# Expert weights read in runs of 8192 bytes, and eight instead of four weight pieces loaded ahead of the routing, in other memory

## The chip, the core and the metric

One Trainium2 chip, one of its cores. The metric is the device time of one execution in microseconds (us). One core has a matrix engine (TensorE: PE in the rows, PEld its weight loads), a vector engine (DVE), a scalar engine (ACT), GpSimd (POOL), and a sync engine (SP), whose queue here only issues DMAs. DMAs of SP and ACT, and those of POOL, run on 16 DMA engines; the rows call SP's queue q1, ACT's q10 and POOL's q0.

## What is computed

A decoder block for 512 tokens of width 1024 in float32: a mixer (a state-space branch and a block-sparse attention branch, merged by gates), then a layer of 32 experts of which each token uses four. Only the second half and its beginning matter here:

```python
h2 = (rms_norm(x, ffn_pre_g[l]) * (1.0 + sc_f) + sh_f).astype(dtype)
logits = hf @ router_w + router_b
top_val, top_idx = lax.top_k(logits, TOP_K)          # 4 of 32 experts
top_w = jax.nn.softmax(top_val, axis=-1)
g = xb @ w_gate[e] + b_gate[e]                       # xb: an expert's tokens
u = xb @ w_up[e] + b_up[e]
g = jnp.minimum(g, SWIGLU_LIMIT)
u = jnp.clip(u, -SWIGLU_LIMIT, SWIGLU_LIMIT)
act = g * jax.nn.sigmoid(SWIGLU_ALPHA * g) * (u + 1.0)
y = act @ w_down[e] + b_down[e]                      # summed per token, times top_w
```

Each of the three matrices of an expert is 1024 x 1024 in float32, 4 MB; the 32 experts together have 403 MB, and every one of them is read once.

## The kernel before

**Stages.** The mixer runs first, up to the output projection with `w_out`. That projection reads the merged branches from `hTh` and `hTl` (two tiles of 16 KB in each of the 128 partitions, in which the modulated input had lain; the pool `front`) and `w_out` itself, split into high and low parts in the tiles `hi` and `lo` (pool `split`, four buffers of each, 4 KB in a partition). Then come the residual (written to `x1d` in HBM by POOL), the modulated input of the experts (`hs`, written to `h2d` by POOL), the router, the top four, and the lists of tokens per expert. Then the expert stage.

**Expert stage.** Each expert is a *slot*. The order of slots is written out in `ORDER`; letters stand for the number of token places that a slot has room for: q is 32, h 64, m 64 + 32, w 128, b 128 + 32 or 128 + 64 (three b, two w, nine each of m, h and q). The first two slots are q slots of experts 0 and 1, whatever the routing says; all others take the expert with a given rank by number of tokens, whose number the SP queue reads from the tile `eid` (`Slot.weight`) once the routing is known.

**Pieces.** A 4 MB matrix is read in four *pieces* of 1 MB, each 256 rows: partition p gets row 256q + p and row 256q + 128 + p, that is two runs of 4096 bytes. `Stream` hands the pieces out in the order in which TensorE wants them (`jobs`): gate and up of slot 0, gate of slot 1, down of slot 0, up of slot 1, gate of slot 2 and so on, 384 pieces in all. Pieces 0 to 19 belong to experts 0 and 1. A piece goes to one of 11 ring buffers in turn (`big_chunk`): buffers 0 to 2 are pairs of tiles of 4 KB from the pool `ring` and take two DMAs of 512 KB each; buffers 3 to 6 (`ring2`), 7 and 8 (`ring3`) and 9 and 10 (`ring4`) are one tile `[128, 2, 1024]` and take one DMA of 1 MB. Line 1134 issues the former, line 1138 the latter. `Stream.get` refills a buffer when its piece has been used.

**Ahead of the routing.** Four pieces, at the places in `PLACES`, are loaded by `early_chunk` (line 1145) into tiles that the wide slots use only later (`EARLY` names them; they come from the pool `slot`, which reuses the memory of the stages before). Nine more go to ring buffers 0 to 8; the two in `ring3` are issued by POOL. The two buffers of `ring4` lie where tiles of the routing lay, so their loads wait for those.

**Use of a piece.** For a slot with at most 64 places the piece is TensorE's moving operand at full precision (line 1287), 32 places working in four column groups side by side, 64 in two. For 128 places it is split into high and low parts by ACT and DVE (lines 110, 111) and multiplied in three passes (lines 115 to 117). The other operand holds the slot's tokens, gathered from `h2d` by an indirect DMA of POOL (`xg`, line 1225) and transposed by TensorE, 128 columns at a time (`Slot.transposed`, lines 1245 and 1255); the activations before `w_down` are transposed in the same way. Results are added to `yd` in HBM by an indirect DMA of POOL (line 1331).

**The end.** `yd` and `x1d` are read back, normed, and written out.

Of the kernel before, what the change touches and what calls it, by code (L numbers as in the profile page):

```python
# [8 lines left out]
F32 = mybir.dt.float32  # L9
F32R = mybir.dt.float32r  # L10
# [7 lines left out]
P = 128  # L18
D = 1024
SEQ = 512  # L20
NT = SEQ // P
DC = D // P
# [12 lines left out]
HALF = P // 2  # L35
# [12 lines left out]
RINGS = 11  # L48
FIRST = 9
MIX = "aagaasstt"  # L50
PLACES = (0, 1, 3, 4)
LOADS = 1
PRIO = 300
EARLY = (("s128", "u128"), ("xh", "xl"), ("ah", "al"), ("xg128", "yo128"))
ALPHA = 1.702
LIMIT = 7.0
SILU_MAX = ALPHA * LIMIT / (1.0 + math.exp(-ALPHA * LIMIT))
# [13 lines left out]
def tile_hybrid_block(ctx: ExitStack, tc: tile.TileContext, A, out):  # L71
    nc = tc.nc
    vec, act, pool, pe = nc.vector, nc.scalar, nc.gpsimd, nc.tensor
# [3 lines left out]
    split = ctx.enter_context(tc.tile_pool(name="split", bufs=4))  # L77
# [9 lines left out]
    def mm_tile():  # L87
        return psum.tile([P, 512], F32, name="mm", tag="mm", bufs=4)

    def ax_tile():  # L90
        return psum.tile([P, 512], F32, name="ax", tag="ax", bufs=3)
# [72 lines left out]
    ident = cst.tile([P, P], F32, name="ident")  # L164
# [354 lines left out]
    for a in range(8):  # L519
        pt = ax_tile()[:64]  # L520
# [3 lines left out]
        for b in range(2):  # L524
            o = U[64 * b:64 * b + 64, 4 * a:4 * a + 4]
# [367 lines left out]
    pos_fix = keep.tile([P, NT, NFIX], F32, name="pos_fix")  # L893
# [130 lines left out]
    for m in (32, HALF):  # L1024
        c = part_col[m] = mo.tile([P, 1], F32, name=f"part{m}")
# [22 lines left out]
    for kh in range(2):  # L1048
        ws = w_chunk(wov, 0, kh)
        for k in range(4):  # L1050
            kk = 4 * kh + k
            for i in range(NT):
                c = slice(i * P, (i + 1) * P)
# [34 lines left out]
    for i in range(NT):  # L1088
        p = mm_tile()
        c = slice(i * P, (i + 1) * P)  # L1090
# [3 lines left out]
    with tc.manual_schedule(engines={vec.engine}):  # L1094
        for c in STEPS.split():
            i = int(c[1])
# [7 lines left out]
    fr.close()  # L1104
    fps.close()

    slp = ctx.enter_context(tc.tile_pool(name="slot", bufs=1, side="right", reuse_waits="tile"))
    ring3 = ctx.enter_context(tc.tile_pool(name="ring3", bufs=FIRST - 7, side="right", reuse_waits="tile"))

# [8 lines left out]
    def tr_tile():  # L1118
        return mps.tile([P, 512], F32, name="tr", tag="tr", bufs=2)
# [20 lines left out]

    def early_chunk(src, tags, eng):

        w = [slp.tile([P, D], F32, name="early", tag=t) for t in tags]
        for k in range(2):
            eng.dma_start(w[k], src[:, k])
        return w
# [4 lines left out]
    def parts_of(m):  # L1151
        return P // m if m <= HALF else 1

    def sized(name, m):

        w = D // parts_of(m)
        return slp.tile([P, w], F32, name=f"{name}{m}", bufs=2 if m <= HALF and name != "u" else 1)

    class Slot:

        def __init__(self, rank, blocks, expert=None):
            self.rank, self.blocks, self.e, self.pick = rank, blocks, expert, None
            if isinstance(expert, int):
                self.pick = own[:, expert:expert + 1].to_broadcast([3 * E + 1, P])
            self.whole = any(m > HALF for m in blocks)
            self.small = any(m <= HALF for m in blocks)
            self.x, self.xg, self.idx, self.w, self.oh = [], [], [], [], []

        def weight(self, name, q):
            if self.e is None:
                self.e = nc.sync.value_load(eid[0:1, self.rank:self.rank + 1], min_val=0, max_val=E - 1)
            w = A[name][0]
            w = w[self.e:self.e + 1] if isinstance(self.e, int) else w[bass.ds(self.e, 1)]
            return w.rearrange("o (k p) n -> p (o k) n", p=P)[:, 2 * q:2 * q + 2]

        def places(self):
            at_ = 0
            place = pos[:, :, self.rank:self.rank + 1] if self.e is None else pos_fix[:, :, self.e:self.e + 1]  # L1180
            for m in self.blocks:
                oh = slp.tile([P, NT, P], BF16, name="oh", bufs=2)
                n = parts_of(m)
                shp = [P, NT, n, m]
                vec.tensor_tensor(oh[:, :, :n * m].rearrange("p i (n m) -> p i n m", n=n),
                                  iota_s[:, None, None, at_:at_ + m].to_broadcast(shp),
                                  place[:, :, None, :].to_broadcast(shp), op=ALU.is_equal)
                self.oh.append(oh[:, :, :n * m])
                at_ += m
# [48 lines left out]
        def transposed(self, t, name, m):  # L1238
            if m <= HALF:
                n = P // m  # L1240
                c = DC // n
                h = slp.tile([P, DC, m], F32, name=f"{name}t{m}", bufs=2)
                pt = tr_tile()[:, :c * P]
                for j in range(c):
                    pe.transpose(pt[:, j * P:(j + 1) * P], t[:, j * P:(j + 1) * P], ident)  # L1245
                act.activation(h.rearrange("p (n j) t -> p j n t", n=n),  # L1246
                               pt.rearrange("p (j n t) -> p j n t", j=c, n=n), AF.Copy)
                return h, None
            h = slp.tile([P, DC, P], F32R, name=name + "h")[:, :, :m]
            l = slp.tile([P, DC, P], F32R, name=name + "l")[:, :, :m]  # L1250
            for q in range(2):
                pt = tr_tile()[:, :4 * m]
                for k in range(4):
                    c = 4 * q + k
                    pe.transpose(pt[:, k * m:(k + 1) * m], t[:m, c * P:(c + 1) * P], ident[:m, :m])
                pv = pt.rearrange("p (k t) -> p k t", t=m)
                act.activation(h[:, 4 * q:4 * q + 4], pv, AF.Copy)
                vec.tensor_sub(l[:, 4 * q:4 * q + 4], pv, h[:, 4 * q:4 * q + 4])
            return h, l
# [48 lines left out]
        def gate(self, ps):  # L1308
            self.s = []
            for p, m in zip(ps, self.blocks):  # L1310
                s = sized("s", m)
                pv, _, sv = self.shaped(p, s, m)
                act.activation(sv, pv, AF.Silu, scale=ALPHA)
                self.s.append(s)
# [20 lines left out]
    class Stream:  # L1335
# [7 lines left out]
        def load(self, tags=None, at_=0, eng=None):  # L1343
            slot, name, q = self.todo.pop(at_)
            w = slot.weight(name, q)
            if tags:
                return slot, 0, early_chunk(w, tags, eng or nc.sync)
            self.live += 1
            return slot, 1, big_chunk(w, eng or nc.sync)
# [45 lines left out]
    with tc.high_priority(PRIO):  # L1395
        parts = {n: stream.load(t, n - i) for i, (n, t) in enumerate(zip(PLACES, EARLY))}

# [13 lines left out]
    rank = rtp.tile([E, 1], F32, name="rank")  # L1411
# [16 lines left out]
    pos = mo.tile([P, NT, E], F32, name="pos")  # L1428
# [17 lines left out]
    pt = tr_tile()  # L1446
# [74 lines left out]
    with tc.For_i(0, n_more, 1):  # L1521
        hit = slp.tile([P, E], F32, name="hit")
        j = slp.tile([P, E], F32, name="hit_j")
# [43 lines left out]
        nc.sync.dma_start(y[:, 0], yd[i * P:(i + 1) * P])  # L1567
    sums, r = [], []
    for i, y in enumerate(ys):
        j = slp.tile([P, D], F32, name="yj", tag=("s128", "yo128")[i % 2])  # L1570
        if i % 2 == 0:
            sums.append(slp.tile([P, 2], F32, name="fs", bufs=2))
        act.activation(j, y[:, 0], AF.Square, accum_out=sums[-1][:, i % 2:i % 2 + 1])
# [30 lines left out]
```

## Time and profile before

| | us |
|---|---|
| median of 3 runs (1586.89 to 1588.97) | 1587.94 |
| the profiled execution | 1585.03 |
| its span, first to last instruction | 1583.2 |
| PE busy in the span | 1400.6 |
| DVE, ACT, POOL busy | 666.3, 441.1, 232.9 |
| DMA queue of SP (q1), share of 16 engines' span | 75.5% |

Busy times are sums over the whole span; the stages have different limits, and a busy PE is not a PE at its peak, since its matmuls are pipelined and a record may last while the next is already running. The DMA share of a stretch can go over 1.00, because an engine's next packet starts a little before the last one ends. HBM was read at 319 GB/s on average over the span; from about 520 us on, where the experts run, it is about 400.

### The profile page before, as it was taken

The page shows a single profiled execution, that of the slowest core. Times are in us where ns is not written, and L with a number is a line of the kernel's source. Part 1 is how long each engine was busy: PE and PEld are TensorE (multiplying, and loading weights), DVE is VectorE, ACT ScalarE, POOL GpSimd, SP SyncE. Part 2 cuts the span into 40 slices and gives each one's busy share as a digit, 9 for nine tenths or more (in the row PEclk, how much of TensorE's full clock was granted, in tenths as well). Part 3 has the DMA queues.
Part 4 walks back from the last instruction along what each step waited for, and adds up shares of the span by engine and source line. Part 5 has one row for each costly group of instructions (what it writes and reads, how often), then busy time and mean ns, then how long its engine had stood idle before and what let it go on. Part 6 is the DMA issues. An engine that isn't in the chain of part 4 may idle for free. (4 is left out here: it accounts for less than half of the span.)

```text
span 1583.2 us, 25206 instructions
## 1 busy us (share of the span) xinstructions
PE 1400.6 (88%) x9746; PEld 748.1 (47%) x9746; DVE 666.3 (42%) x1435; ACT 441.1 (28%) x715; POOL 232.9 (15%) x241
## 2 busy tenths in 40 slices
PE   6999898899895899799999979997998999999871
PEld 3877676556673433233543336435533556333220
DVE  4697898586746210113431025304512556111003
ACT  4444343455432101003230123304302344010001
POOL 1000334000335101011011111101110111010101
PEclk9999999899996999999999999998998999899985
DMA  9524554542647999999999999999999999999995
GB/s 317 164 67 158 175 184 137 172 157 90 222 176 263 377 405 399 397 404 400 403 343 399 394 401 406 397 400 400 395 402 400 406 394 402 395 397 403 401 404 202
DMA packets 160458, 506.96 MB, mean 320 GB/s; under 512 B 18789, under 2 KB 21481, under 8 KB 160079
## 3 DMA queue, kind: packets, MB, share of 16 engines
q1 hardware_dynamic: 140208, 461.04, 75.5%
q0 software_dynamic: 11456, 26.81, 6.4%
q10 hardware_dynamic: 8670, 17.46, 3.2%
q8 instruction: 78, 1.28, 0.3%
q14 instruction: 46, 0.37, 0.1%
HBM read 481.93 MB, written 23.33 MB: 319 GB/s over the span
## 5 line engine op out<-in xcount | busy, mean ns | idle before, releaser
L1287 PE MATMUL acc<-raw,xt 128*32 128x256 f32 (+1 forms) x3712 | 467.7, 463 | 43.7 <-DMA raw<-in_w_up 22.2
L1287 PEld LDWEIGHTS acc<-raw,xt 128*32 128x32 f32 (+1 forms) x3712 | 145.4, 119 | 295.4 <-issue 200.7
L1287 PE MATMUL acc<-raw,at 128*32 128x256 f32 (+1 forms) x1888 | 233.6, 465 | 19.5 <-DMA raw<-in_w_down 19.3
L111 DVE TENSOR_TENSOR lo<-raw,hi 128x1024 fp32r<-128x1024 f32 x170 | 208.3, 1251 | 79.2 <-ACT hi L110 77.6
L110 ACT ACTIVATE hi<-raw 128x1024 fp32r<-128x1024 f32 x170 | 175.7, 1057 | 120.7 <-PE acc L117 36.3
L1321 DVE TENSOR_SCALAR u<-acc 128x256 f32<-128x256 f32 (+2 forms) x44 | 27.6, 628 | 394.8 <-PE acc L1287 373.6
L1331 POOL DMA_INDIRECT yd<-yo,dst x44 | 74.0, 1682 | 562.6 <-ACT yo L1330 458.7
L1287 PEld LDWEIGHTS acc<-raw,at 128*32 128x32 f32 (+1 forms) x1888 | 74.6, 120 | 149.0 <-issue 93.7
L1225 POOL DMA_INDIRECT xg<-h2d,src x44 | 48.8, 1109 | 371.9 <-DVE tb_t L1229 163.0
L1330 ACT ACTIVATE yo<-acc,w 128x256 f32<-128x256 f32 (+2 forms) x44 | 26.9, 636 | 230.6 <-PE acc L1287 197.2
L1246 ACT ACTIVATE at<-tr 128x256 f32<-128x256 f32 (+1 forms) x39 | 18.1, 487 | 251.9 <-PE tr L1245 251.9
L115 PE MATMUL mm<-hTh,hi 128*128 128x512 f32 x192 | 79.1, 416 | 9.5 <-ACT stage L741 7.0
L115 PE MATMUL acc<-hi,xh 128*128 128x512 f32 x160 | 74.5, 465 | 12.6 <-ACT hi L110 12.6
L117 PE MATMUL mm<-hTh,lo 128*128 128x512 f32 x192 | 77.6, 409 | 5.7 <-DVE lo L111 5.7
L116 PE MATMUL mm<-hTl,hi 128*128 128x512 f32 x192 | 78.0, 406 | 0.0
L116 PE MATMUL acc<-lo,xh 128*128 128x512 f32 x160 | 67.1, 419 | 3.8 <-DVE lo L111 3.8
L1246 ACT ACTIVATE xt<-tr 128x256 f32<-128x256 f32 (+1 forms) x39 | 18.0, 487 | 175.3 <-PE tr L1245 175.3
L117 PE MATMUL acc<-hi,xl 128*128 128x512 f32 x160 | 65.7, 410 | 0.0
L255 DVE SCALAR_TENSOR_TENSOR acc<-raw,cond,acc 128x512 f32<-128x512 f32 x56 | 57.1, 1020 | 0.5
L115 PE MATMUL mm<-hi,hTh 128*128 128x512 f32 x128 | 52.6, 415 | 2.2 <-DVE ga L863 1.3
L117 PE MATMUL mm<-hi,hTl 128*128 128x512 f32 x128 | 51.9, 405 | 1.1 <-DVE hTl L308 1.1
L116 PE MATMUL mm<-lo,hTh 128*128 128x512 f32 x128 | 51.6, 403 | 0.0
(577 smaller groups left out, 1815.7 us busy)
## 6 DMA issues: line engine op xcount, KB each, us to landing
raw<-in_w_up SPq DMA_DIRECT2D x97, 1024.0 KB, 16.4
raw<-in_w_gate SPq DMA_DIRECT2D x88, 1024.0 KB, 16.7
raw<-in_w_down SPq DMA_DIRECT2D x88, 1024.0 KB, 16.1
raw<-in_w_down SPq DMA_DIRECT2D x78, 512.0 KB, 15.8
raw<-in_w_gate SPq DMA_DIRECT2D x72, 512.0 KB, 16.4
raw<-in_w_up SPq DMA_DIRECT2D x60, 512.0 KB, 15.8
raw<-in_ada_w SPq DMA_DIRECT2D x48, 512.0 KB, 4.6
raw<-in_w_in SPq DMA_DIRECT2D x32, 512.0 KB, 4.7
```

The costliest lines, as they stand in the source:

```text
L110: act.activation(hv, src, AF.Copy)
L111: eng.tensor_sub(lv, src, hv)
L115: pe.matmul(o, sh, mh, start=start, stop=False)
L116: pe.matmul(o, sh, ml, start=False, stop=False)
L117: pe.matmul(o, sl, mh, start=False, stop=stop)
L255: vec.scalar_tensor_tensor(acc, w[:, k % 2], cond[:, k:k + 1], acc, op0=ALU.mult, op1=ALU.add)
L1225: pool.indirect_dma_start(out=xg[:r], out_offset=None, in_=h2d.rearrange("t (n c) -> (t n) c", n=n), in_offset=bass.IndirectOffsetOnAxis(a ...
L1246: act.activation(h.rearrange("p (n j) t -> p j n t", n=n), pt.rearrange("p (j n t) -> p j n t", j=c, n=n), AF.Copy)
L1287: pe.matmul(o, xh[:, kk], raw[:, c], start=(kk == 0), stop=last)
L1321: vec.tensor_scalar(uv, pv, LIMIT + 1.0, 1.0 - LIMIT, op0=ALU.min, op1=ALU.max)
L1330: act.activation(yv, pv, AF.Copy, scale=w)
L1331: pool.indirect_dma_start(out=yd.rearrange("t (n c) -> (t n) c", n=parts_of(m)), out_offset=bass.IndirectOffsetOnAxis(ap=idx[:, :1], axis= ...
```

## The change

Two parts. First, the rows of a piece are dealt out differently: partition p now gets rows 256q + 2p and 256q + 2p + 1, which are neighbours in HBM, so that a tile of `ring2` to `ring4` is filled by runs of 8192 bytes. Buffers 0 to 2 and the early tiles, which take a row per DMA, keep runs of 4096 bytes. The tokens and the activations are transposed to match: each transpose takes every second column (`rows_of_k`). Second, eight pieces, 3 to 10, are loaded early in place of pieces 0, 1, 3 and 4: four into the `hi` and `lo` tiles, and four into the tiles of the wide slots, which now have a pool of their own, `block`, opened first on the side of the memory where `hTh` and `hTl` lay. The new attribute `fixed` tells the two fixed slots from the others in `places`.

```diff
-PLACES = (0, 1, 3, 4)
+PLACES = (3, 4, 5, 6, 7, 8, 9, 10)
-EARLY = (("s128", "u128"), ("xh", "xl"), ("ah", "al"), ("xg128", "yo128"))
+EARLY = (("hi", "lo"),) * 4 + (("s128", "u128"), ("xh", "xl"), ("ah", "al"), ("xg128", "yo128"))
...
+    blp = ctx.enter_context(tc.tile_pool(name="block", bufs=1, side="right", reuse_waits="tile"))
     slp = ctx.enter_context(tc.tile_pool(name="slot", bufs=1, side="right", reuse_waits="tile"))
...
-        w = [slp.tile([P, D], F32, name="early", tag=t) for t in tags]
+        w = [(split if t in ("hi", "lo") else blp).tile([P, D], F32, name="early", tag=t) for t in tags]
...
+    def rows_of_k(t, m, k):
+        c = 2 * P * (k // 2) + k % 2
+        return t[:m, c:c + 2 * P - 1:2]
...
-            return w.rearrange("o (k p) n -> p (o k) n", p=P)[:, 2 * q:2 * q + 2]
+            return w.rearrange("o (q p c) n -> q p (o c) n", q=4, c=2)[q]
...
-                    pe.transpose(pt[:, j * P:(j + 1) * P], t[:, j * P:(j + 1) * P], ident)
+                    pe.transpose(pt[:, j * P:(j + 1) * P], rows_of_k(t, P, j), ident)
...
-                    pe.transpose(pt[:, k * m:(k + 1) * m], t[:m, c * P:(c + 1) * P], ident[:m, :m])
+                    pe.transpose(pt[:, k * m:(k + 1) * m], rows_of_k(t, m, c), ident[:m, :m])
```

The tiles of 128 places (`s128`, `u128`, `xh`, `xl`, `ah`, `al`, `xg128`, `yo128`) move from `slot` to `block` everywhere else too.

**On SP, where the early pieces are issued.** The first row of each listing is the last ring piece ahead of them. Names after "waits" are what the queue waits for: DMAHW an earlier DMA of SP or ACT, DMASW one of POOL, the others an engine. Before:

```order
123 L1134 DMA raw<-in_w_up 128x1024 [waits DMAHW6_49,DVE_49,Activation_49]
124 L1145 DMA early<-in_w_gate 128x1024 [waits DMASW1_49,DMAHW1_49,DVE_49,DMAHW7_49,PE_49,Activation_49]
125 L1145 DMA early<-in_w_gate 128x1024 [waits DMAHW0_49,DVE_49]
126 L1145 DMA early<-in_w_gate 128x1024 [waits DMASW0_49]
127 L1145 DMA early<-in_w_gate 128x1024 [waits DMAHW2_49,DMASW7_49]
128 L1145 DMA early<-in_w_gate 128x1024 [waits DMAHW3_49]
129 L1145 DMA early<-in_w_gate 128x1024 [waits DMAHW4_49,DVE_49,PE_49]
130 L1145 DMA early<-in_w_up 128x1024 [waits DMAHW5_49,Pool_49]
```

And now:

```order
123 L1136 DMA raw<-in_w_gate 128x1024 [waits DMAHW6_49,DVE_49,Activation_49]
124 L1147 DMA early<-in_w_gate 128x1024 [waits DMAHW7_49,PE_49]
125 L1147 DMA early<-in_w_gate 128x1024 [waits DMAHW0_49,PE_49]
126 L1147 DMA early<-in_w_up 128x1024 [waits DMAHW1_49,PE_49]
127 L1147 DMA early<-in_w_up 128x1024 [waits DMAHW2_49]
128 L1147 DMA early<-in_w_up 128x1024 [waits DMAHW3_49,PE_49]
129 L1147 DMA early<-in_w_up 128x1024 [waits DMAHW4_49]
130 L1147 DMA early<-in_w_up 128x1024 [waits DMAHW5_49,PE_49]
```

DMAs of POOL and the engines DVE, ACT and POOL are gone from the waits; PE is left, beside an earlier DMA of the queue. The early DMAs go on to row 139, sixteen in all.

**On SP, right behind them.** Before, the two pieces for `ring4` (rows 132 and 133) come next, then refills of the ring:

```order
131 L1145 DMA early<-in_w_up 128x1024 [waits DMAHW6_49]
132 L1138 DMA raw_4582<-in_w_down 128x2x1024 [waits DMAHW7_49,DVE_49,PE_49]
133 L1138 DMA raw_4584<-in_w_down 128x2x1024 [waits DMASW4_49,DMASW3_49,DMASW5_49,DMASW2_49,DMASW6_49,DVE_49,DMAHW0_49,PE_49,Activation_49]
134 L1134 DMA raw<-in_w_down 128x1024 [waits DMAHW1_49,PE_49]
135 L1134 DMA raw<-in_w_down 128x1024 [waits DMAHW2_49,PE_49]
136 L1134 DMA raw<-in_w_up 128x1024 [waits DMAHW3_49,PE_49]
```

Now five reads of expert numbers stand ahead (rows 140 to 149), then a refill of ring buffer 0, and only then the two for `ring4`:

```order
148 L1181 TENSOR_LOAD eid
149 L1181 ISA x2
150 L1136 DMA raw<-in_w_up 128x1024 [waits DMAHW7_49,PE_49]
151 L1136 DMA raw<-in_w_up 128x1024 [waits DMAHW0_49,PE_49]
152 L1140 DMA raw_4601<-in_w_up 128x2048 [waits DVE_49,DMAHW1_49,Activation_49,Pool_49]
153 L1140 DMA raw_4603<-in_w_up 128x2048 [waits DMASW3_49,DMASW4_49,DMASW2_49,DMASW5_49,DMASW1_49,DMASW6_49,DMASW0_49,DMAHW2_49,DVE_49,Activation_49]
154 L1136 ISA
```

The first piece for `ring4` has moved behind a DMA that waits for PE. The shape of a 1 MB load, 128x2x1024 before, is 128x2048.

## Rows read from the trace of the kernel before

**Rows 1.** The page, part 2: the span in 40 slices.
```profile
GB/s 317 164 67 158 175 184 137 172 157 90 222 176 263 377 405 399 397 404 400 403 343 399 394 401 406 397 400 400 395 402 400 406 394 402 395 397 403 401 404 202
```
**Rows 2.** DMA queues, 540 to 790 us: packets, MB, share of 16 engines.
```profile
q1 hardware_dynamic: 25260, 95.90, 95.8%
q0 software_dynamic: 2179, 4.33, 6.9%
```
**Rows 3.** SP's waits, 560 to 1550 us: total us, times, longest.
```profile
SPq L1138 <- PE acc L1287: 102.8, 63, 5.6
SPq L1138 <- DMA raw<-in_w_gate: 91.3, 71, 3.8
```
**Rows 4.** PE's groups, 540 to 1550 us: busy us, mean ns, idle before.
```profile
L1287 PE MATMUL acc<-raw,xt 128*64 128x512 f32 x1216 | 302.2, 612 | 19.7 <-DMA raw<-in_w_gate 10.4 <-DMA raw<-in_w_up 9.0
L1287 PE MATMUL acc<-raw,xt 128*32 128x256 f32 x2304 | 159.8, 391 | 21.9 <-DMA raw<-in_w_up 11.1 <-DMA raw<-in_w_gate 10.6
L1287 PE MATMUL acc<-raw,at 128*64 128x512 f32 x608 | 150.2, 615 | 10.4 <-DMA raw<-in_w_down 10.1
L1287 PE MATMUL acc<-raw,at 128*32 128x256 f32 x1200 | 81.9, 392 | 7.9 <-DMA raw<-in_w_down 7.9
```
**Rows 5.** Stretches: busy us of PE, PEld, DVE, ACT, POOL (count), PEclk, DMA share, GB/s.
```profile
805.00:810.00 5.00, 5.00 (x23) 2.78 (x22) 3.06 (x3) 2.01 (x2) 0.00 (x0) 1.00 0.93 355
810.00:815.00 5.00, 5.00 (x22) 2.82 (x21) 0.00 (x0) 0.00 (x0) 0.00 (x0) 1.00 0.76 266
815.00:820.00 5.00, 5.00 (x58) 2.30 (x60) 0.00 (x0) 1.80 (x2) 1.62 (x1) 1.00 0.69 218
```
**Rows 6.** The same view, before and at the start of the expert stage.
```profile
455.00:475.00 20.00, 18.73 (x93) 15.19 (x91) 9.82 (x25) 4.90 (x12) 12.71 (x29) 1.00 0.08 33
...
500.00:515.00 15.00, 8.09 (x52) 4.99 (x52) 6.59 (x34) 1.87 (x6) 3.60 (x4) 0.54 0.71 275
515.00:520.00 5.00, 4.46 (x72) 2.46 (x75) 3.18 (x12) 1.37 (x2) 0.00 (x0) 1.00 0.63 207
```
**Rows 7.** SP's timeline: start us, us, merged issues.
```profile
482.29 11.91 SPq L1145 DMA_DIRECT2D early<-in_w_gate  x6
...
506.83 10.90 SPq L1138 DMA_DIRECT2D raw<-in_w_down  x2
```
**Rows 8.** SP's waits, the whole run.
```profile
SPq L1145 <- DMA x1d<-X: 29.5, 1, 29.5
```
**Rows 9.** PE's timeline: last reading of `hTl`, and the first pieces.
```profile
470.64 0.40 PE L117 MATMUL mm<-hi,hTl 128*128 128x512 f32 x1
...
514.24 1.07 PE L1453 MATMUL tr<-perm,wdT 32*128 32x32 f32 x8
515.24 1.07 PE L1287 MATMUL acc<-early,xt 128*32 128x256 f32 x16
```
**Rows 10.** DMA queues, 16 to 20 us (runs of 2048 bytes).
```profile
DMA packets 810, 1.56 MB, mean 391 GB/s; under 512 B 47, under 2 KB 47, under 8 KB 810
q1 hardware_dynamic: 810, 1.56, 105.4%
```
**Rows 11.** DMA queues, 541 to 551 us (4096 bytes, nearly alone).
```profile
DMA packets 1074, 4.15 MB, mean 415 GB/s; under 512 B 64, under 2 KB 64, under 8 KB 1073
q1 hardware_dynamic: 1073, 4.13, 102.3%
```
**Rows 12.** DMA queues in two loads `sg<-gd`, 299.5 to 301.5, 305 to 307 us.
```profile
q10 hardware_dynamic: 100, 0.82, 100.5%
...
q10 hardware_dynamic: 102, 0.84, 101.3%
```
**Rows 13.** DMA queues, 304.5 to 308 us.
```profile
q10 hardware_dynamic: 132, 0.95, 68.3%
```
**Rows 14.** Transposes of narrow slots (line 1245): ns min/median/max, times.
```profile
L1245 PEld LDWEIGHTS tr<-ident,xg x116: 137/140/224, 509.5 to 1507.9; 128*128 128x128 f32 x116
L1245 PE MATMUL tr<-ident,s x116: 272/273/476, 526.6 to 1540.9; 128*128 128x128 f32 x116
```

More of the change, by code (lines that the diff above doesn't have):

```diff
@@ L1156, in sized @@
         w = D // parts_of(m)
-        return slp.tile([P, w], F32, name=f"{name}{m}", bufs=2 if m <= HALF and name != "u" else 1)
+        return (slp if m <= HALF else blp).tile([P, w], F32, name=f"{name}{m}", bufs=2 if m <= HALF and name != "u" else 1)
+    def rows_of_k(t, m, k):
+        c = 2 * P * (k // 2) + k % 2
+        return t[:m, c:c + 2 * P - 1:2]
     class Slot:
         def __init__(self, rank, blocks, expert=None):
-            self.rank, self.blocks, self.e, self.pick = rank, blocks, expert, None
+            self.rank, self.blocks, self.e, self.fixed, self.pick = rank, blocks, expert, expert, None
             if isinstance(expert, int):
@@ L1175, in weight @@
             w = w[self.e:self.e + 1] if isinstance(self.e, int) else w[bass.ds(self.e, 1)]
-            return w.rearrange("o (k p) n -> p (o k) n", p=P)[:, 2 * q:2 * q + 2]
+            return w.rearrange("o (q p c) n -> q p (o c) n", q=4, c=2)[q]
         def places(self):
             at_ = 0
-            place = pos[:, :, self.rank:self.rank + 1] if self.e is None else pos_fix[:, :, self.e:self.e + 1]
+            place = pos[:, :, self.rank:self.rank + 1] if self.fixed is None else pos_fix[:, :, self.fixed:self.fixed + 1]
             for m in self.blocks:
@@ L1248, in transposed @@
                 return h, None
-            h = slp.tile([P, DC, P], F32R, name=name + "h")[:, :, :m]
-            l = slp.tile([P, DC, P], F32R, name=name + "l")[:, :, :m]
+            h = blp.tile([P, DC, P], F32R, name=name + "h")[:, :, :m]
+            l = blp.tile([P, DC, P], F32R, name=name + "l")[:, :, :m]
             for q in range(2):
@@ L1569, in tile_hybrid_block @@
     for i, y in enumerate(ys):
-        j = slp.tile([P, D], F32, name="yj", tag=("s128", "yo128")[i % 2])
+        j = blp.tile([P, D], F32, name="yj", tag=("s128", "yo128")[i % 2])
         if i % 2 == 0:
```

## The prediction

> **What bounds the kernel now.** I read the slices of the whole span first, then stretches of the expert stage, then the waits of the two engines that meet there, SP and PE, and at last the 70 us in which the mixer ends and the experts begin.
>
> From the fifteenth slice on the rate stands near 400 GB/s in every slice but the twenty-first and the last [rows 1]: the expert stage, some 1030 of 1583 us, is paced by the reading of weights. In a long stretch SP's queue and POOL's together take 102.7% of the 16 engines, so there is no idle engine to fill; SP's queue carries 95.90 MB in 250 us, 383.6 GB/s, or **2.73 us for a piece** of 1 MB [rows 2]. SP waits for PE to release a buffer and for its own earlier DMAs in like measure [rows 3], which alone would leave open who paces whom. PE decides it: it stands idle for weights at all four kinds of its slots' matmuls, 19.7 + 21.9 + 10.4 + 7.9 = 59.9 us [rows 4]. The one place where it is the other way round is the widest slot: from 805 to 820 us PE is busy throughout and the DMA share falls to 0.93, 0.76 and 0.69; against the 1.03 of full reading [rows 2] that is 3.6 us lost [rows 5]. So the kernel ends when the weights are read, and what shortens it is more bytes moved before the stage, or a higher rate in it.
>
> Ahead of the stage there is room: from 455 to 475 us the DMA share is 0.08, from 500 to 515 us 0.71, from 515 to 520 us 0.63 [rows 6]. SP has nothing to issue because its next DMAs, the early pieces, wait until 482.29 us [rows 7], 29.5 us of it for the store of `x1d` to have read the residual, in whose memory the early tile lies [rows 8]. The tiles that the change uses instead are last read by the output projection's matmul at 470.64 us [rows 9].
>
> **Early pieces.** The new queue shows only PE among the engines that they wait for. So they start at about 471 us, 11 us sooner. Eight pieces are 8.39 MB; with three stores of `x1d` (1.57 MB) that is 9.96 MB, at 415 GB/s [rows 11] 24 us, to 495 us, and the four stores of `h2d` (2.1 MB, 5 us) end at about 500, as they do now. The routing chain therefore finds the engines as it finds them today, and I cost its delay at nothing; its cover is that the ring cannot refill before PE starts anyway. By 500 us four pieces more have landed: 4 x 2.73 = 10.9 us.
>
> One is given back. The first piece for `ring4` goes out at 506.83 us today [rows 7]; now it stands behind a refill of ring buffer 0, hence behind PE's reading of piece 0, which ends just after the routing's last transposes, 514.24 + 1.07 = 515.3 us [rows 9]. POOL's two pieces keep their place. So at 515.3 us three pieces more are there, 8.2 us. From then on SP can issue the refill, both `ring4` pieces, and a refill for each of pieces 1 and 2 as PE goes through them at 1.07 us a piece [rows 9]: five pieces, 13.7 us of reading, against 8 x 1.07 = 8.6 us in which PE lives on early pieces and releases no ring buffer. No bubble, and the 0.40 of 5 us that are idle now between 515 and 520 [rows 6] are mostly used, worth 1.3 us. **9.5 us** in all; 5.5 if another piece is displaced, 11 if none is. The five reads of expert numbers run while SP has to wait in any case.
>
> **Runs of 8192 bytes.** The trace has packets of three sizes. Of 2048 bytes: 810 - 47 small = 763 in 4 us x 16 x 1.054, 88.4 ns each [rows 10]. Of 4096 bytes, with POOL's queue silent: 1009 in 10 us x 16 x 1.023, 162.2 ns [rows 11]. Of 8192 bytes, in two loads of the mixer's gates (`sg<-gd`, 1 MB each, runs of 8192 bytes): 202 in two stretches of 2 us, 16 x 2 x (1.005 + 1.013) = 64.6 us, 319.7 ns [rows 12]. Two of 4096 cost 324.4. So the long packet saves 4.7 ns by its own rows; a straight line through the two shorter ones (2048 bytes cost 73.8 ns) would put it at 309.8, saving 14.6; and over the whole second load, its edges and the other queue's packets included, it takes 329.7 (0.95 MB, 116 packets, 68.3% of 16 x 3.5 us) [rows 13], a loss of 5.3. The bounds are thus 309.8 and 329.7. I take 317: a quarter of the way from the size's own rows to the line, since those rows come from loads too short to keep all engines full.
>
> After 515 us 384 - 17 = 367 pieces are left; 8 of 11 go to tiles with long runs, 267. One ns per packet is worth 128 / 16 / 1.03 x 267 = 2.07 us. At 317: 7.4 x 2.07 = **15.3 us**; 9.7 by the size's own rows, 30.3 by the line, a loss of 11 at 329.7.
>
> [...]
>
> **The rest.** The widest slot: over the 30 us or so in which PE sets the pace, reading 2.3% faster gains nothing; 0.7 us back. The transposes read every second word; no row shows that, so between nothing and a doubling of both their parts, 0 to 140 + 273 ns for each of 2 x 116 + 2 x 40 = 312 of them [rows 14] (the 80 are those of the wide slots, of like length). They end on PE, whose idle 59.9 us cover up to 0.19 us each; I take nothing, because a read at half rate would bear on the 140 ns alone. Buffers 0 to 2 keep packets of 4096 bytes and cost what they do.
>
> **Sum.** The profiled execution took 1585.03 us: - 9.5 - 15.3 + 0.7 gives 1560.9. The median of the runs lies 2.9 above that execution, so I forecast **1563.8 us** for the median, rounded to 1564. The least change that a measurement of this kernel can tell from none is about 0.2%, 3.2 us.
>
> **Rivals.**
> *B, long runs bring nothing.* If something other than a cost per packet holds the engines at 415 GB/s, only the early pieces count: 1585.0 - 9.5 + 2.9 = 1578.4. For it: 4096-byte packets reach 415 GB/s and the 8192-byte ones 410 and 418 (0.82 and 0.84 MB in 2 us). Against it: the busy time per byte fell from 2048 to 4096 bytes and, by 1.4%, once more. [...]
> *C, the line holds.* 30.3 instead of 15.3: 1548.8. 0.07, since the size's own rows contradict it.
> *D, PE becomes the bound.* Place: the 312 transposes. If both parts double, 129 us are added; 59.9 are covered: 1585.0 - 9.5 + 69 + 2.9 = 1647. It decides from 0.19 us more each. Against it: only one operand is read with gaps. 0.04.
> *E, long packets cost what they cost beside another queue.* At 329.7 ns the 11 us lost eat the early gain: 1585.0 - 9.5 + 11 + 2.9 = 1589.4. From 328.8 ns on there is no gain; from 331 on the change is slower by over 0.2%. For it: POOL's queue is active through the stage, 6.9% [rows 2]. Against it: rows 12. 0.09, of which a third is slower.
>
> **How the numbers follow.** The forecast has 0.64, and by the bounds of its terms (5.5 to 11; 9.7 to some 20) a range of its own from 1556 to 1574. With B and the near half of C the range is 1551 to 1580; D, E and the rest of C are left out, below 0.2. Faster: 0.64 + 0.16 + 0.07 = 0.87. E and D share the rest: 0.06 same, 0.07 slower.
>
> **What would show it.** Sixteen early DMAs, the first issued near 471 us; a DMA share near 1 from there to about 500; PE's first piece still near 511 us. In the stage some 35,000 packets fewer on SP's queue, and a piece in about 2.68 us. The transposes at 273 ns. Wrong would be: a stretch without POOL traffic that still moves 415 GB/s (B); early DMAs that wait for anything but PE; PE's waits for weights gone (D).

## The result, and the profile after

The change takes **1566.2 us** (median of 4 runs, 1561.0 to 1568.4) where the kernel before took 1587.4 beside it: ratio 0.9864, 95% interval [0.9835, 0.9892]. In a second set of runs the ratio was 0.9856 [0.9831, 0.9882]. The forecast was 1564, in a range from 1551 to 1580. The profiled execution took 1565.9 us (span 1564.2), so it stands for the median.

The slices of the whole span, part 2 of its page, answer to [rows 1]:

```profile
GB/s 324 161 70 148 181 189 142 155 142 98 199 222 323 316 414 406 405 411 405 413 314 409 406 404 411 404 408 407 415 397 407 415 393 411 402 406 411 409 412 202
```

From the fifteenth slice on the rate stands some 2% higher. The thirteenth (some 470 to 510 us) rose from 263 to 323 GB/s: the early pieces. The fourteenth fell from 377 to 316, so that the two together read the same; this execution's mixer ended later, and the account below starts from its end for that reason. The twenty-first, the widest slot, fell from 343 to 314. DMA queues from 540 to 790 us [rows 2]:

```profile
DMA packets 19137, 101.88 MB, mean 408 GB/s; under 512 B 2203, under 2 KB 2971, under 8 KB 10331
...
q1 hardware_dynamic: 16796, 97.15, 94.5%
q0 software_dynamic: 2321, 4.46, 7.2%
```

97.15 MB in 250 us are 388.6 GB/s, or 2.70 us for a piece; it was 2.73, the forecast 2.68. Over the whole run SP's queue carries 105,696 packets in place of 140,208, 34,512 fewer (forecast some 35,000). Of all packets 19137 - 10331 = 8806 have 8192 bytes; less the 20 that are in neither queue, 8786 are SP's, 71.97 MB, and the rest of its bytes are 6147 packets of 4096. With 162.2 ns for each of these [rows 11], 997 us, the remaining 2783 us of engine time (16 x 250 x 0.945 = 3780) give **316.7 ns for a long packet**; forecast 317. Ten microseconds without POOL's packets show both lengths bare, first the kernel before (1400 to 1410 us), then the change (1000 to 1010 us):

```profile
DMA packets 1069, 4.09 MB, mean 409 GB/s; under 512 B 70, under 2 KB 70, under 8 KB 1069
```

```profile
DMA packets 583, 4.24 MB, mean 424 GB/s; under 512 B 67, under 2 KB 67, under 8 KB 67
```

So 409 to 415 GB/s [rows 11] are no ceiling. Of all stretches of 10 us between 560 and 1540 us that hold no packet of POOL, those of the widest slot aside, the kernel before has twenty, at 406 to 416 GB/s; the change has four with long packets alone, at 423 to 425. PE's groups from 540 to 1550 us [rows 4]:

```profile
L1295 PE MATMUL acc<-raw,xt 128*64 128x512 f32 x1216 | 299.0, 608 | 13.5 <-DMA raw<-in_w_gate 8.3 <-DMA raw<-in_w_up 5.0
L1295 PE MATMUL acc<-raw,xt 128*32 128x256 f32 x2332 | 159.9, 389 | 17.6 <-DMA raw<-in_w_up 10.5 <-DMA raw<-in_w_gate 6.8
L1295 PE MATMUL acc<-raw,at 128*64 128x512 f32 x608 | 148.8, 611 | 8.8 <-DMA raw<-in_w_down 8.6
L1295 PE MATMUL acc<-raw,at 128*32 128x256 f32 x1216 | 80.8, 384 | 5.6 <-DMA raw<-in_w_down 3.7 <-SPq L1529 1.9
```

PE is still short of weights at all four kinds of matmul, 45.5 us in place of 59.9 (in 1.9 of it SP's queue, and not a piece, came last): reading still sets the pace. SP's timeline around the routing [rows 7] (start us, length, merged issues):

```profile
472.81 0.80 SPq L1147 DMA_DIRECT2D early<-in_w_gate  x2
474.44 6.16 SPq L1147 DMA_DIRECT2D early<-in_w_up  x8
481.55 8.47 SPq L1147 DMA_DIRECT2D early<-in_w_gate  x6
517.49 4.21 SPq L1136 DMA_DIRECT2D raw<-in_w_up  x2
521.87 1.58 SPq L1140 DMA_DIRECT2D raw<-in_w_up  x2
```

The sixteen early DMAs go out from 472.81 us on, and nothing of them waits for `x1d` any more. The first `ring4` piece stands behind the refill of ring buffer 0, at 521.87 us; it went out at 506.83 before. Stretches, with the columns of [rows 5]; the first five answer to [rows 6], the last three to [rows 5]:

```profile
455.00:475.00 20.00, 20.00 (x87) 16.10 (x87) 9.20 (x20) 4.15 (x13) 8.00 (x20) 1.00 0.32 107
475.00:500.00 25.00, 16.75 (x110) 13.09 (x108) 16.25 (x37) 11.06 (x24) 18.38 (x35) 0.91 1.01 397
500.00:515.00 15.00, 5.40 (x31) 3.43 (x31) 11.77 (x54) 1.28 (x5) 6.37 (x14) 0.50 0.56 211
515.00:520.00 5.00, 5.00 (x28) 2.90 (x26) 0.00 (x0) 0.59 (x1) 0.00 (x0) 0.50 1.00 397
520.00:525.00 5.00, 5.00 (x58) 2.48 (x61) 2.97 (x12) 0.16 (x1) 0.00 (x0) 0.70 0.61 204
800.00:805.00 5.00, 5.00 (x22) 2.66 (x20) 3.04 (x3) 1.06 (x1) 0.00 (x0) 1.00 0.78 279
805.00:810.00 5.00, 5.00 (x23) 2.74 (x24) 0.00 (x0) 0.00 (x0) 0.00 (x0) 1.00 0.66 219
810.00:815.00 5.00, 5.00 (x63) 2.33 (x64) 0.00 (x0) 1.80 (x2) 1.62 (x1) 1.00 0.63 203
```

The transposes of the narrow slots [rows 14]:

```profile
L1253 PEld LDWEIGHTS tr<-ident,xg x116: 194/209/219, 513.2 to 1489.6; 128*128 128x128 f32 x116
...
L1253 PE MATMUL tr<-ident,s x116: 272/283/489, 532.4 to 1522.5; 128*128 128x128 f32 x116
```

Their weight load grew from 140 to 209 ns, the matmul from 273 to 283.

**Where the time went.** Two profiled executions can't be laid over each other by the clock on the wall, since their mixers end at different times. As a common mark I take the first transpose of the mixer's output `hs`, here first in the kernel before, then in the change:

```profile
L950 PE MATMUL ax<-ident,hs x32: 272/273/475, 470.9 to 486.8; 128*128 128x128 f32 x32
```

```profile
L950 PE MATMUL ax<-ident,hs x32: 272/273/476, 477.1 to 493.0; 128*128 128x128 f32 x32
```

From the mark to the end the kernel before takes 1583.2 - 470.9 = 1112.3 us, the change 1564.2 - 477.1 = 1087.1 (1085.4 in a second profile). So 25 to 27 us are gained behind the mark, and in this execution 6.2 lost ahead of it; the whole times differ by 21 to 23. Four stretches from the mark on, 70, 160, 150 and 600 us long, of the kernel before and of the change:

```profile
470.90:540.90 70.00, 44.93 (x516) 28.74 (x514) 34.34 (x118) 16.99 (x38) 27.20 (x48) 0.83 0.77 284
540.90:700.90 160.00, 140.59 (x1218) 49.75 (x1220) 18.62 (x76) 13.17 (x28) 18.11 (x14) 0.97 1.03 401
700.90:850.90 150.00, 146.18 (x1032) 65.74 (x1028) 48.20 (x93) 39.37 (x51) 17.28 (x12) 1.00 1.01 386
850.90:1450.90 600.00, 559.03 (x4270) 265.84 (x4268) 196.28 (x386) 153.87 (x204) 71.84 (x50) 0.97 1.03 399
```

```profile
477.10:547.10 70.00, 52.15 (x554) 32.32 (x552) 34.21 (x118) 17.10 (x38) 27.04 (x48) 0.80 0.89 346
547.10:707.10 160.00, 147.61 (x1290) 54.53 (x1287) 22.30 (x91) 13.77 (x29) 19.09 (x15) 0.98 1.02 409
707.10:857.10 150.00, 145.11 (x1008) 66.66 (x1010) 49.21 (x99) 40.01 (x53) 17.60 (x13) 1.00 0.98 384
857.10:1457.10 600.00, 568.13 (x4354) 271.20 (x4346) 193.02 (x374) 154.43 (x206) 71.52 (x50) 0.98 1.02 407
```

The last column, turned into time at 400 GB/s, gives an account: 70 x (346 - 284) / 400 = **10.9 us** in the first stretch (the early pieces), 160 x 8 / 400 = 3.2 in the second, -0.8 in the third, where the widest slots lie and PE sets the pace, 600 x 8 / 400 = 12.0 in the fourth (the long runs, **14.4 us** in all). Together 25.3. The column is rounded to 1 GB/s, which alone can move the fourth term by 1.5 us, and the last 107 us are not in it; so the close fit to 25.2 is in part chance.

### The profile page after: what moved, and what is told of

It reads as the page before. It is cut to its first block, busy times and chain, and to the rows that moved or that the text cites. A ratio compares the mean times of both kernels' runs of the same rounds, so it can differ in the third digit from the quotient of the medians.

```text
span 1564.2 us, 25215 instructions
## 1 busy us (share of the span) xinstructions
PE 1400.5 (90%) x9746; PEld 755.8 (48%) x9746; DVE 665.6 (43%) x1435; ACT 440.4 (28%) x715; POOL 231.0 (15%) x241
## 3 DMA queue, kind: packets, MB, share of 16 engines
q1 hardware_dynamic: 105696, 461.04, 74.7%
## 5 line engine op out<-in xcount | busy, mean ns | idle before, releaser
L1295 PE MATMUL acc<-raw,xt 128*32 128x256 f32 (+1 forms) x3648 | 461.5, 464 | 31.6 <-DMA raw<-in_w_up 15.5
L1295 PE MATMUL acc<-raw,at 128*32 128x256 f32 (+1 forms) x1888 | 229.3, 457 | 14.4 <-DMA raw<-in_w_down 12.3
```

Source lines behind the costliest of these rows:

```text
L1295: pe.matmul(o, xh[:, kk], raw[:, c], start=(kk == 0), stop=last)
```

## The experiments

All ratios are to the kernel before, run on the same chip; 0.1% is 1.6 us. GB/s are those of the four stretches from each kernel's own mark.

**The two parts alone.** The early pieces without the runs:

```diff
-            return w.rearrange("o (q p c) n -> q p (o c) n", q=4, c=2)[q]
+            return w.rearrange("o (k p) n -> p (o k) n", p=P)[:, 2 * q:2 * q + 2]
-        c = 2 * P * (k // 2) + k % 2
-        return t[:m, c:c + 2 * P - 1:2]
+        return t[:m, k * P:(k + 1) * P]
```

> The change without its 8192-byte runs: the rows of a weight piece are dealt as before (two runs of 4096 bytes per partition) and the transposes read neighbouring columns again; the eight early pieces stay. Theory (two independent gains): the early pieces alone bring 9.5 us by the prediction (5.5 to 11), up to 11.6 us by the bytes read at equal distance from the mixer's end in the trace of the change; so a ratio of 0.993 to 0.994 to the kernel before, a rate near 400 GB/s in the expert stage, some 140,200 packets on SP's queue, and weight loads of the transposes back at 140 ns. Rival (the start of the stage was hidden anyway, all 21 us come from the runs): ratio 0.999 to 1.001.

Measured: 1577.9 us, 0.9942 [0.9924, 0.9961], **9.2 us** less by the ratio (6.2 to 12.1). The first and the last stretch:

```profile
470.20:540.20 70.00, 52.16 (x548) 32.85 (x548) 34.22 (x118) 17.12 (x38) 27.46 (x48) 0.78 0.86 333
...
850.20:1450.20 600.00, 559.98 (x4266) 265.11 (x4262) 193.92 (x379) 154.46 (x205) 71.85 (x50) 0.97 1.03 399
```

The gain lies in the first 70 us, 8.6 us by this row; in the last stretch, as in the second, the rate is that of before to the GB/s. From the mark to the end it takes 1104.2 us, 8.1 less than before. The rival falls.

The runs without the early pieces: the kernel before, with the new line of `weight` and `rows_of_k`, run twice.

> The kernel before with the 8192-byte runs and the strided transposes alone: four early pieces, waits and tiles as before. Theory: 267 + a few pieces with 64 packets fewer on each pair of runs save 7.4 ns per long packet, 15 us less 0.7 at the widest slot, or what is left of the measured 21 us beside the early pieces, 10 to 14 us: ratio 0.991 to 0.994; stretches with long runs alone at about 424 GB/s, those with short runs at 409 to 412. Rival (the rate is set elsewhere): ratio 0.999 to 1.001. Rival (the saving per packet is that of the straight line, 14.6 ns): 30 us, ratio 0.981.

> The runs alone once more, for a second profile and a closer interval. In the first, the bytes read by 59 us after the mixer's end lay 1.9 MB (4.8 us) behind those of the kernel before, with PE at a granted clock of 0.62 and a DMA share of 0.41 in the 10 us in which it ate the early pieces. Theory (that gap is of the execution: PE came out of the routing at the low clock, and with it the release of buffers): another clock there, another gap, and from 850 us on again some 13 us gained. Rival (the gap belongs to the runs): the same 1.9 MB behind again. The ratio to the kernel before again 0.991 to 0.996.

Measured: 1577.4 us, 0.9937 [0.9912, 0.9962], and again 1576.5 us, 0.9917 [0.9900, 0.9934]: **10 to 13 us** less, inside what the theory gave, and far from the 30 us of the line. The first stretch of the two profiles, then the last of the first profile:

```profile
478.20:548.20 70.00, 45.03 (x478) 30.67 (x476) 33.41 (x116) 16.25 (x36) 27.12 (x48) 0.76 0.70 255
...
858.20:1458.20 600.00, 568.78 (x4334) 273.85 (x4330) 197.43 (x395) 155.63 (x208) 73.27 (x51) 0.97 1.02 406
```

```profile
474.50:544.50 70.00, 48.25 (x516) 31.85 (x514) 33.65 (x117) 17.02 (x38) 26.93 (x48) 0.78 0.76 278
```

The same program read 255 GB/s there once and 278 the other time, 5.1 and 1.1 us behind the 284 of the kernel before. The gap of the first profile is thus mostly of the execution. It goes with PE's granted clock where PE eats the early pieces: in the 10 us from 44.1 us behind the mark on, PE was busy throughout in both, with 94 matmuls at a mean clock of 0.62 and a DMA share of 0.41 in the first profile, 142 at 0.80 and 0.74 in the second. A PE that gets through fewer matmuls releases fewer buffers; that this is the cause is argued from these rows, no run sets the clock.

By whole times the parts add up: 9.2 + 10 to 13 are 19 to 22 us, the change gains 22 to 23 by its two ratios. By the profiles they do not: behind the mark the parts alone gain 8.1 and 9.3 or 11.2 us, together 17 to 19, the change 25 to 27. Most of what is missing lies in the first stretch, where the profiles of the parts stand at a clock of 0.76 to 0.78 and those of the change at 0.80 and 0.83; whether the parts also help each other there is not shown.

The early part halved (`PLACES = (3, 4, 5, 6)`, `EARLY = (("hi", "lo"),) * 4`, short runs):

> The early part halved, with short runs and neighbouring columns as before: only the four early pieces in the tiles of high and low parts, none in the block tiles, and at places 3 to 6. They start some 11 us sooner than the four of the kernel before, and are as many. Theory (what counts is the number of pieces that lie ready when PE starts, not when their reading begins): no gain, ratio 0.998 to 1.002, since the first ring4 piece stands behind a refill as in the change. Rival (the sooner start is the gain, all 9 to 11 us of it): ratio 0.993 to 0.994.

Measured: 1585.1 us, 0.9986 [0.9971, 1.0001]. Its first stretch:

```profile
472.30:542.30 70.00, 49.23 (x516) 31.92 (x514) 33.91 (x118) 17.09 (x38) 27.25 (x48) 0.78 0.74 281
```

281 GB/s against 284: the earlier start brings nothing that shows. It is not quite alone in this run, since the first `ring4` piece has moved behind the refill here too, which the prediction priced at one piece, 2.7 us. The four pieces more that fit before PE starts do bring something: 333 - 281 GB/s x 70 us are 3.6 MB of their 4.2.

The change itself, on the chip of this run and of `all_long2` and `places` below:

> The change as it is, on the chip of the three below, as their measure and as a second profile: ratio 0.984 to 0.989 to the kernel before. It also shows whether the 6 us by which the mixer ended later in the first profile of the change belong to the change (then again near 477 us) or to that execution (then anywhere from 470 to 480 us, as in the profiles of the first four experiments); from the mixer's end to the end of the kernel 1085 to 1089 us in either case.

Measured: 1564.8 us, 0.9856 [0.9831, 0.9882]; mark at 478.2 us, 1085.4 us from there to the end. The later mark came back, which I take up below.

**More long packets.** Ring buffers 0 to 2 as pairs, two ways (the first takes pairs from a pool of three in turn; the second holds three pairs for the whole kernel):

```diff
+    pairs = [ring.tile([P, 2, D], F32, name=f"raw{i}", tag=f"raw{i}") for i in range(3)]
...
-            w = [ring.tile([P, D], F32, name="raw") for _ in range(2)]
-            for k in range(2):
-                eng.dma_start(w[k], src[:, k])
-            return w
...
+            w = pairs[halves[0] % 6 // 2]
...
+            eng.dma_start(w, src)
+            return [w[:, k] for k in range(2)]
```

> The change with ring buffers 0 to 2 as pairs in one tile, so that all eleven buffers are read with runs of 8192 bytes; the mixer takes halves of such pairs, which moves some of its instructions. Theory (the gain goes with the number of long packets): about 100 pieces more, 7.4 ns x 128 packets x 100 / 16 / 1.03 = 5.7 us less than the change in the stretch from the mixer's end to the end of the kernel, some 12,800 packets fewer on SP's queue, 420 to 424 GB/s in every stretch without POOL's packets; ratio to the kernel before near 0.983 if the mixer ends when it does now. Rival (the rate in mixed stretches is already at its limit, or PE is the bound by now): no gain after the mixer's end.

Measured: 1569.7 us (1560.2 to 1579.4), 0.9888 [0.9854, 0.9922]. The mark lies at 487.9 us. I put that down to the mixer's own loads, which now wait for whole pairs; the run below, which holds its pairs, has the mark at 475.9, but no row isolates it. Behind the mark it takes 1079.6 us, 7.5 and 5.8 less than the two profiles of the change (expected 5.7). Second and fourth stretch:

```profile
557.90:717.90 160.00, 145.84 (x1276) 54.34 (x1272) 21.81 (x88) 14.66 (x31) 20.09 (x16) 0.99 1.02 412
...
867.90:1467.90 600.00, 569.83 (x4356) 274.35 (x4348) 194.26 (x376) 155.62 (x207) 71.88 (x51) 0.98 1.02 409
```

None, eight and all of eleven buffers with long runs give 401, 409 and 412 GB/s in the second stretch, 399, 407 and 409 in the fourth: the rate goes with the number of long packets, as the theory wants. The rows are dealt alike in the change and here; buffers 0 to 2 took them in packets of 4096 bytes there, so the new dealing without long packets had not brought this last step. Beyond that, length and the order in which HBM is read are not told apart: no run reads the whole stage in the new dealing with short packets. The highest of the 40 slices of `all_long` (39 us each, POOL's packets among them) shows 420 GB/s, where from the fifteenth on the change's reach 415 and those of the kernel before 406.

> All eleven buffers with 8192-byte runs once more, now with the three pairs of ring 0 to 2 held for the whole kernel, and the mixer's loads dealt to their halves in turn. The first such kernel took 1079.6 us from the mixer's end to its own end where the change took 1087.1, but its mixer ended 11 us later. Theory: again 1078 to 1082 us behind the mixer's end, 420 to 424 GB/s in stretches without POOL's packets; the mixer within 5 us of the change's, so a ratio of 0.981 to 0.984 to the kernel before. Rival (the mixer's loads in an order of their own cost what the runs save): ratio 0.985 to 0.992.

Measured: **1557.0 us**, 0.9807 [0.9784, 0.9830], 7.7 us less than the change on the same chip and the best version of this study. Its profile has the mark at 475.9 us and 1084.0 behind it (expected 1078 to 1082, so a miss), with only 336 GB/s in the first stretch at a clock of 0.78.

**What the strided transposes cost.** `rows_of_k` with 128 neighbouring columns, the weights' rows as in the change, so that rows and columns no longer belong together and only the time counts:

> The change with its transposes reading 128 neighbouring words instead of every second one; the rows of the weights then meet the wrong columns of the tokens, so that the expert part of the output is another one. It prices the strided read. In the trace of the change the weight load of a transpose grew from 140 to 209 ns and its matmul from 273 to 283 ns. Theory (PE is idle 44 us for weights and the load lies beside it): 140 and 273 ns again, and the time of the change within 0.15%, ratio to the kernel before 0.985 to 0.988. Rival (312 transposes delay what PE does next, 79 ns each): 25 us less, ratio near 0.971.

Measured: 1562.1 us, 0.9835 [0.9814, 0.9857], a little below the 0.985 to 0.988 expected; the interval overlaps both of the change, and behind the mark it takes 1086.0 us against 1087.1 and 1085.4. A cost of the gaps of a few us is not excluded, one of 25 us is. The weight load is back at 140 ns:

```profile
L1252 PEld LDWEIGHTS tr<-ident,xg x116: 137/140/224, 516.3 to 1491.5; 128*128 128x128 f32 x116
```

Each transpose made twice (`for _ in range(2):` ahead of both `pe.transpose`):

> The change with each of its 312 transposes in the expert stage made twice, the second over the first. It asks what covers PE's work there: 312 x 283 ns = 88 us more for PE, against the 44 us in which PE is idle for weights. Theory (the idle time for weights is the cover, and the change's 79 ns more per transpose, 25 us in all, lay inside it): part of the 88 us is swallowed, the kernel takes 44 to 66 us more than the change (ratio to the kernel before 1.013 to 1.028), and PE's waits for weights fall to a few us. Rival (transposes stand on the path, nothing covers them): 88 us more, ratio 1.041 or above. Rival (a second weight load of 209 ns adds to the 283 ns): 153 us of work, ratio 1.055 or above.

Measured: 1567.4 us, 0.9862 [0.9843, 0.9882], the ratio of the change; behind the mark 1091.1 us, 4 to 6 more than its two profiles. So the doubling costs a few us at most, and none of the three expectations hit. Part 1 of the page, first of the change, then of this kernel:

```profile
PE 1400.5 (90%) x9746; PEld 755.8 (48%) x9746; DVE 665.6 (43%) x1435; ACT 440.4 (28%) x715; POOL 231.0 (15%) x241
```

```profile
PE 1425.9 (91%) x10058; PEld 792.2 (51%) x10058; DVE 666.1 (43%) x1435; ACT 441.1 (28%) x715; POOL 231.5 (15%) x241
```

All 312 are there, but PE is busy only 25.4 us longer, 81 ns for each. That is a net figure: the rows of the transposes themselves went from 56.0 to 94.1 us (122 ns for each), while PE's other groups took 12.7 us less. Either way matmuls behind one another overlap, so counts times 283 ns was a wrong price, mine. Most of the 25 us fits into PE's idle time for weights, as the theory said of the cover. PE's groups from 500 to 1560 us, change and this kernel:

```profile
L1295 PE MATMUL acc<-raw,xt 128*32 128x256 f32 (+1 forms) x3648 | 461.5, 464 | 31.6 <-DMA raw<-in_w_up 15.5 <-DMA raw<-in_w_gate 15.1 <-ACT xt L1254 0.5
```

```profile
L1297 PE MATMUL acc<-raw,xt 128*32 128x256 f32 (+1 forms) x3648 | 456.1, 463 | 19.5 <-DMA raw<-in_w_up 13.8 <-DMA raw<-in_w_gate 5.3 <-issue 0.5
```

The idle time fell from 31.6 to 19.5 us here, and from 14.4 to 10.2 at the matmuls of `w_down`, 16.3 in all.

**The order of the early pieces** (`PLACES = (0, 1, 3, 4, 6, 7, 9, 10)`):

> The change with its early pieces at places 0, 1, 3, 4, 6, 7, 9, 10 in place of 3 to 10, so that PE meets a ring piece after every two early ones; on SP's queue half of the first refill then stands behind the two ring4 pieces. Theory (between 515 and 525 us the change leaves the DMA engines idle for some 2 us because PE eats early pieces and releases nothing, and for the displaced ring4 piece): the gap shrinks, 1 to 3 us less from the mixer's end to the end of the kernel than the change's 1087. Rival (SP's queue is in order and the ring4 pieces wait for the routing's memory, so that the refill behind them is late instead): the same time or up to 3 us more.

Measured: 1565.2 us, 0.9851 [0.9828, 0.9875], the time of the change; 1089.7 us behind the mark, 329 GB/s in the first stretch at a clock of 0.78. The 1 to 3 us less behind the mark did not come, rather the rival's up to 3 more; whether the order gave something that the low clock took back can't be told apart here.

**The mixer's end.** From the last product of attention and values (line 802) to the mark, three profiles with the rows of the weights dealt as before (the kernel before, `early_only`, `four_hilo`) took 470.9 - 386.1 = 84.8, 85.0 and 84.7 us; all eleven with the new rows 87.8 to 92.5, the change 477.1 - 389.3 = 87.8 and 88.1. Line 802 before and in the change:

```profile
L802 PE MATMUL ax<-PT,V x160: 272/273/476, 290.5 to 386.1; 128*64 128x128 f32 x160
```

```profile
L802 PE MATMUL ax<-PT,V x160: 272/273/477, 290.5 to 389.3; 128*64 128x128 f32 x160
```

The change and `early_only` differ only in the rows of the weights and the transposes of the expert stage. SP is reading the first ring pieces in this stretch while ACT's queue loads the gates `ga`. DVE's wait for them, over the 22 us from some 40 us behind that product on (total, times, longest), before and in the change:

```profile
DVE ga L863 <- DMA ga<-gd: 3.9, 2, 2.3
```

```profile
DVE ga L863 <- DMA ga<-gd: 8.5, 2, 7.8
```

So I let the four `ring2` pieces of the first lap be read in short runs again:

```diff
+        if turn[0] is not None and turn[0] < 7:
+            for k in range(2):
+                eng.dma_start(w[:, k], src[:, k])
+        else:
+            eng.dma_start(w, src)
```

> The change with the first four ring2 pieces, read while the mixer still runs, in two DMAs each of 4096-byte runs; every later lap keeps its 8192-byte runs. From the last product of attention and values to the first transpose of the mixer's output the profiles with short runs took 84.7, 84.8 and 85.0 us, the seven with long runs 87.8 to 92.5. Theory (in that stretch the pieces lie beside the small loads of ACT's queue, `ga` with 2048-byte packets, then `rwt` and `X`; an engine that takes packets of both queues in turn gives the queue with the long packets the larger share, so ga lands later and DVE waits 7.8 us for it in place of 2.3): with short packets there again the stretch takes 84.5 to 85.5 us, and the kernel 3 to 5 us less than the change, ratio near 0.982. Rival (the stretch differs by the clock of the execution, chance among ten profiles): 84.5 to 92.5, ratio 0.985 to 0.987. Rival (it is the four DMAs more on SP's queue): 85 to 92, same ratio.

Measured: 1563.3 us, 0.9835 [0.9813, 0.9857]; the mark at 475.5, 87.9 us behind the product at 387.6. The wait stayed:

```profile
DVE ga L863 <- DMA ga<-gd: 8.5, 2, 7.1
```

The theory of packet lengths falls. And the wait was no good sign to begin with: with the rows dealt as before, `early_only` and `four_hilo` show

```profile
DVE ga L863 <- DMA ga<-gd: 6.8, 2, 6.2
...
DVE ga L863 <- DMA ga<-gd: 6.6, 2, 6.0
```

and took 85.0 and 84.7 us, like the kernel before with its 2.3; `all_long2`, with the new rows, waits 3.0 at the longest and took 88.5. That the long packets get the larger share is in the traces all the same: where both queues had work, about as many packets of the one went as of the other, 211 of SP's (0.86 MB) and 209 of ACT's (0.79 MB) from 445 to 449 us in the kernel before, 44 of SP's (0.34 MB, 42 of them of 8192 bytes) and 42 of ACT's (0.09 MB) from 433 to 434 us in the change. That this delays the mixer's end no run shows. The four pieces still read every second row per DMA, so the new dealing of rows itself is left as a cause, or chance; it stays open. The time may be 1 to 3 us better than the change's, but the intervals overlap.

> The kernel with long runs in all eleven buffers and pairs held for the whole kernel, with all seven pieces that SP reads ahead of the mixer's end in short runs, for the reason of the run before. Theory: 1 to 4 us less than the 1557 measured without this (its mixer is another order of instructions, so the stretch is not the same), ratio 0.978 to 0.981. Rival: no difference, 0.9807.

Measured: 1559.4 us, 0.9813 [0.9793, 0.9833]. No difference, as the rival had it.

## Why the prediction was right

- **What bounds the kernel.** Reading, before and after: PE's waits for weights fell but stayed, and 25 us more of PE's work moved the end by a few us at most.
- **Early pieces, -9.5 us.** Alone 9.2 by the ratio, 10.8 between the medians; in the change's first stretch 10.9 and 12.6 in its two profiles. The bounds 5.5 and 11 had left out the 1.3 us of the sum; with it a piece less or more gives 6.8 and 12.2. The order of events was as told: waits for PE alone, the `ring4` piece behind the refill. Three details were off. The first DMA left 4.3 us ahead of the mark, where I had put it at the last reading of `hTl`, right at the mark; the first tiles of `hi` and `lo` come free before that matmul. PE's first piece, "still near 511", came at 514.40, 37.3 us behind the mark, where 510.69 had been 39.8 behind it: the early pieces no longer lie beside the gather of `xg`, on which PE had waited 2.7 us and now does not wait (DMA share 0.13 from 510 to 512 us). And "no bubble" was wrong: from 520 to 525 us the share is 0.61, with PE at a granted clock of 0.50 from 515 to 520 and of 0.70 on average from 520 to 525 us. It had been at 0.50 since 500 us, where PE was busy for 5.40 of 15 us. I had priced PE's pieces at 1.07 us, 16 matmuls at a clock of 1.00; from 520.26 us on, 30 took 3.25 us. What the early pieces bring goes with that clock: of the ten profiles with eight early pieces, five at a mean of 0.78 in the first stretch show 329 to 340 GB/s there, two at 0.80 show 341 and 346, three at 0.83 to 0.85 show 352 to 356. The 9.5 was thus met in part by luck: a bubble that I had excluded stands against a routing that ran 2.5 us sooner.
- **Long runs, -15.3 us.** 316.7 ns against 317; the size's own rows and the line were the right pair of bounds. Behind the first stretch they bring 3.2 - 0.8 + 12.0. That the term comes out so close is partly luck. In the stretch of [rows 2] itself the short packets took 163.7 ns (16 x 250 x 0.958 us / 23,413), and with that the long ones in the change come to 315.7, a saving of 11.7 ns in place of 7.4, worth 24 us by the prediction's own factor. Against it, the share of the two queues, which the sum held at 1.03, fell from 1.027 to 1.017, by an estimate 10 us, 1% of the stage's 1030. With all buffers long the rate of the second stretch stands 2.7% higher than before, 412 / 401 GB/s.
- **Widest slot, +0.7 us.** Too small. The whole third stretch gained nothing, 386 to 384 GB/s (381 to 386 in three profiles with short runs, 378 to 385 in eleven with long ones), and the loss from 800 to 815 us grew from 3.6 to some 5 us: 5 x (1.02 - 0.78 + 1.02 - 0.66 + 1.02 - 0.63) / 1.02.
- **Transposes, 0.** Right in time, and in the main in reason: the gaps bore on the 140 ns, which grew by half, and on the matmul, which I had left out, with 10 ns. `contig` and `twice` show that PE's idle time covers this to within a few us.
- **The sum.** Forecast for the stage 24.1 us, measured 25 to 27. The step that was missing is the mixer, whose time I left as it was. The sum for the profiled execution was 1560.9, and it took 1565.9: the mark came 6.2 us later, 3.2 of them before the last product of attention and values, with nothing changed there, and 3.0 behind it, where all profiles of the new rows lose as much or more; the first part is within what executions differ by (385.0 to 390.1 us in eleven profiles with the same mixer), the cause of the second is open. 1.1 us gained more than forecast stand against that. The medians, 1566.2 and 1564.8, lie 2.4 and 1.0 above 1563.8.
- **Rivals.** B, the 0.16 in the sum of chances, falls with the 424 GB/s of a bare stretch. C falls with 316.7 ns, E with the same beside POOL's 7.2%, D with 209 and 283 ns where it needed a doubling, and with the doubled transposes.

## What to carry to other kernels

Where weights are read without a break, count what lies loaded when the reader starts, not when loading began: as many pieces, four, begun some 11 us sooner were worth nothing that could be told from none, four pieces more 9 us. Price a longer packet from the rows of every size in the trace, and expect the gain only where the DMA engines set the pace (here 399 to 407 GB/s in the fourth stretch, but 386 to 384 in the third, where PE was busy for 146 and 145 of 150 us). Compare two profiles from a common mark in the program, since the same program's mark stood at 478.2 us in one execution and at 474.5 in the next, and look at PE's granted clock where the stages meet before a difference there is put down to the change.

## What the runs showed of the hardware

- A weight load of 128 x 128 float32 that reads every second word took 209 ns in place of 140, the matmul with it 283 in place of 273.
- A second transpose of 128 x 128 float32 right behind the first adds 122 ns to the transposes' own busy time and 81 ns net to PE's, not 283.
- On SP's queue runs of 8192 bytes go as packets of 8192 (8786 of them from 540 to 790 us of the change), at 423 to 425 GB/s in its stretches of 10 us with long packets alone and none of POOL's, where those of 4096 reach 406 to 416.
- With PE at a mean granted clock of 0.62 in place of 0.80, the same program read 156 GB/s in place of 265 in the 10 us in which it used the early pieces.
